# A decoder step on one core: gate pairs in seven block products, with all low parts on VectorE

## The chip, the cores and the metric

The kernel runs on one core of a Trainium2 chip. The metric is the device time of one execution in microseconds, the median of several runs. The engines are TensorE (PE, with its weight load PEld), VectorE (DVE), ScalarE (ACT), GpSimd (POOL) and SyncE (SP), whose queue issues most DMAs.

## The reference

One layer of a hybrid decoder for 576 tokens at once: a prompt of 512 and 8 samples of 8 tokens, with the same weights; D = 1024, D_FF = 2816, float32.

```python
x += 0.5 * gate1 * swiglu(mod(rmsnorm(x)), w_ff1_in, w_ff1_out)      # FF1
x += gate2 * W_out(sum_i sigmoid(gate_i(h)) * proj_i(branch_i(h)))   # mixer: windowed attention, SSD, RG-LRU
x += 0.5 * gate3 * swiglu(mod(rmsnorm(x)), w_ff2_in, w_ff2_out)      # FF2
y = rmsnorm(x)

def swiglu(h, w_in, w_out):
    u, v = jnp.split(h @ w_in, 2, axis=-1)
    return (jax.nn.silu(u) * v) @ w_out
```

`mod` scales and shifts by vectors worked out from the condition c and the 9216 columns of `w_ada`. States and key/value rows are outputs too.

## The kernel before, in words

Activations lie transposed: 128 partitions of D by 576 tokens, in 8 tiles `H` (high part, fp32r) and 8 tiles `L` (low part, value minus H). A float32 product is made of three fp32r ones: `wh*H + wl*H + wh*L`, where `wh` is the weight's cast and `wl` the rest.

The program is one list of `Unit`s, which `run` goes through in order. A Unit is a block of 128 weight columns: up to 8 k tiles x 3 passes x 2 token halves of 288, so 48 matmuls of 128x288 (L342) into a PSUM tile of two banks from the pool `mm` (two such tiles). `run` issues the loads of weights ahead on SP's queue (`load`, L170), `split` casts `wh` on ScalarE (L278) and subtracts `wl` on VectorE, or on POOL for 48 units with `pool=True` (L280); a Unit's result is evicted at the start of the next Unit. Between the k tiles `run` steps lanes: generators of other work, such as `ada` (modulation, 1 MB of `w_ada` and 8 matmuls, L593, a step), `prep` (bias tables), norms, attention and scans. The order of all instructions on each engine is the order in which the program is written.

`ff_units` writes a feed-forward: its 22 blocks of D_FF stand in groups of 8, 8 and 6. For each block there is a u Unit (evicted with silu on ScalarE, L724) and a v Unit (multiplied on VectorE, L732, then `split` into `a` by L180 and L181), then for each group 8 out-projection Units (L707, L712, L713 add to x). The first blocks of FF2 are halved, so that they begin while the norm of the second token half is still running.

## Time and profile before

| | |
|---|---|
| median of 3 runs | 2097.17 us (2095.91 to 2100.96) |
| the profiled execution | 2096.72 us |
| its span, first to last instruction | 2094.9 us |
| mean granted TensorE clock | 0.990 |
| busy: TensorE, VectorE, ScalarE, POOL | 97%, 45%, 40%, 13% |
| the chain that ended last | TensorE 65% of the span, L342 alone 53% |

The chain follows the work back from the last instruction, at each step to what released it. FF1 takes about the first 500 us, the mixer 500 to 1630, FF2 the rest. An operation's time is read from the timeline of its engine; the bracket at the end of such a row is the idle time of the engine before it and what ended it. A clock of 1.00 is 2.4 GHz.

### The profile page before, as it was taken

Reading aid. Unit: us, or ns where it says so; the run is one execution under the profiler, and the core shown is the slowest. Engines: PE = TensorE matmul, PEld = TensorE weight load, DVE = VectorE, ACT = ScalarE, POOL = GpSimd, SP = SyncE. Lnnn points to the kernel's source line nnn. Section 1 sums busy time; section 2 is a strip of 40 time slices with the busy share of each in tenths; the row PEclk is TensorE's granted clock in tenths of the full one; section 3 lists DMA queues with packets and bytes.
Section 4 is the critical chain, followed back from the end, with each engine's and each line's share of the span. In section 5 each row is a group of like instructions: output and inputs, shape, how many; then the busy total and the mean of one; then the engine's idle time right before and its main releaser. Section 6 shows DMA issues by size and latency. Waiting matters only on the chain.

```text
span 2094.9 us, 40560 instructions
## 1 busy us (share of the span) xinstructions
PE 2030.4 (97%) x17104; PEld 1911.1 (91%) x17104; DVE 952.2 (45%) x1759; ACT 832.8 (40%) x1508; POOL 271.6 (13%) x351
## 2 busy tenths in 40 slices
PE   7999999998999999999999989999999999999997
PEld 6888999998998899999999878888989799999997
DVE  4323333337568655225353573434445633333343
ACT  5222222137557446125352646555425522122132
POOL 2000000006003211000003131101136300000002
PEclk8999999999999999999999999999999999999999
DMA  9856322235641485332333185788787422222222
GB/s 276 265 158 209 89 82 81 85 92 152 185 141 54 125 264 174 100 112 60 95 94 99 54 249 183 243 269 284 248 277 229 127 81 81 84 89 81 86 84 68
DMA packets 381088, 304.20 MB, mean 145 GB/s; under 512 B 16176, under 2 KB 329126, under 8 KB 380905
## 3 DMA queue, kind: packets, MB, share of 16 engines
q1 hardware_dynamic: 370888, 271.15, 43.4%
q0 software_dynamic: 10016, 30.44, 4.3%
q8 instruction: 135, 2.21, 0.4%
q14 instruction: 49, 0.39, 0.1%
HBM read 269.88 MB, written 31.66 MB: 144 GB/s over the span
## 4 chain that ended last, share of the span: by engine, by line
PE 65%; DVE 6%; DMA 2%; ACT 2%; issue 1%; SPq 1%; POOL 0%; POOLq 0%; DVEq 0%; ACTq 0%
PE mm L342 53%; PE kt L1735 2%; PE S L1723 1%; PE O L1828 1%; SPq L170 1%; PE px_ld L593 1%; PE px_lru L1889 1%; PE sc L1451 1%; PE po L1507 1%; DVE sq L646 1%; DMA cv<-cache_win_kv 1%; DVE wl L280 1%; DMA ck<-cache_win_kv 1%; PE pt L1490 1%; DVE L L699 0%
## 5 line engine op out<-in xcount | busy, mean ns | idle before, releaser
L342 PE MATMUL mm<-H,wh 128*128 128x288 f32 x4112 | 957.4, 305 | 20.2 <-DVE x L713 9.2
L342 PE MATMUL mm<-L,wh 128*128 128x288 f32 x4112 | 918.7, 296 | 2.6 <-DVE L L181 1.5
L342 PE MATMUL mm<-H,wl 128*128 128x288 f32 x4112 | 917.7, 296 | 0.6 <-POOL wl L280 0.6
L342 PEld LDWEIGHTS mm<-H,wh 128*128 128x128 f32 x4112 | 669.6, 189 | 77.2 <-issue 54.0
L342 PEld LDWEIGHTS mm<-L,wh 128*128 128x128 f32 x4112 | 673.0, 188 | 4.8 <-DVE L L181 2.6
L342 PEld LDWEIGHTS mm<-H,wl 128*128 128x128 f32 x4112 | 673.1, 188 | 1.8 <-POOL wl L280 0.8
L280 DVE TENSOR_TENSOR wl<-raw,wh 128x1024 fp32r<-128x1024 f32 (+1 forms) x241 | 289.9, 1206 | 277.8 <-ACT wh L278 260.1
L278 ACT CAST wh<-raw 128x1024 fp32r<-128x1024 f32 (+2 forms) x289 | 289.7, 1009 | 104.0 <-PE mm L342 94.7
L280 POOL TENSOR_TENSOR wl<-raw,wh 128x1024 fp32r<-128x1024 f32 (+2 forms) x48 | 101.3, 2115 | 722.6 <-ACT wh L278 714.1
L707 DVE SCALAR_TENSOR_TENSOR x<-mm,modT,x 128x288 f32<-128x288 f32 (+1 forms) x112 | 50.9, 480 | 163.3 <-PE mm L342 163.3
L724 ACT ACTIVATE su<-mm 128x576 f32<-128x576 f32 x42 | 27.4, 651 | 238.8 <-PE mm L342 238.8
L180 ACT CAST H<-su 128x576 fp32r<-128x576 f32 x44 | 29.6, 674 | 232.6 <-DVE su L732 226.0
L732 DVE TENSOR_TENSOR su<-su,mm 128x576 f32<-128x576 f32 x42 | 31.7, 754 | 142.4 <-PE mm L342 142.4
L1740 ACT COPY KT<-kt 128x512 f32<-128x512 f32 x78 | 45.5, 587 | 76.5 <-PE kt L1735 65.9
L953 DVE SCALAR_TENSOR_TENSOR acc<-raw,v,acc 128x512 f32<-128x512 f32 x120 | 54.3, 523 | 45.6 <-ACT acc L950 45.4
L1735 PE MATMUL kt<-mats,ck 128*128 128x128 f32 x416 | 64.1, 278 | 9.6 <-DMA ck<-cache_win_kv 7.9
L1735 PEld LDWEIGHTS kt<-mats,ck 128*128 128x128 f32 x416 | 51.3, 143 | 11.9 <-DMA ck<-cache_win_kv 8.2
L1483 ACT ACTIVATE lg<-lg,neg 128x128 f32<-128x128 f32 (+1 forms) x96 | 39.9, 417 | 29.5 <-DVE neg L1474 28.4
L1961 DVE TENSOR_TENSOR sg<-sg,mm 128x576 f32<-128x576 f32 x24 | 18.0, 752 | 68.0 <-PE mm L342 41.7
L181 DVE TENSOR_TENSOR L<-su,H 128x576 fp32r<-128x576 f32 x44 | 33.4, 759 | 32.7 <-ACT H L180 32.7
L641 ACT ACTIVATE sq<-x 128x288 f32<-128x288 f32 x48 | 21.3, 443 | 64.2 <-DVE x L713 32.1
L1738 DVE COPY KT<-kt 128x512 f32<-128x512 f32 x26 | 17.9, 690 | 54.6 <-PE kt L1735 47.2
(388 smaller groups left out, 1720.1 us busy)
## 6 DMA issues: line engine op xcount, KB each, us to landing
raw<-w_in SPq DMA_DIRECT2D x96, 512.0 KB
raw<-w_ff_in SPq DMA_DIRECT2D x88, 512.0 KB
ada<-w_ada SPq DMA_DIRECT2D x72, 512.0 KB
...
```

The costliest lines, as they stand in the source:

```text
L180: self.later(delay[0], lambda: nc.scalar.copy(H, src))
L181: self.later(delay[1], lambda: nc.vector.tensor_tensor(out=L, in0=src, in1=H.bitcast(F32), op=ALU.subtract), L)
L278: nc.scalar.copy(H, r)
L280: self.later(0 if i < 4 else 2, lambda: e.tensor_tensor(out=L, in0=r, in1=H.bitcast(F32), op=ALU.subtract), L)
L342: nc.tensor.matmul(ps[:M, hf, :HALF], wt[:, k, :], x[:, hf * HALF:(hf + 1) * HALF], start=(k == 0 and p == 0), stop=(k == nk - 1 and p == 2))
L707: nc.vector.scalar_tensor_tensor(out=x[:, c0:c0 + n], in0=ps[:, hf, 0:n], scalar=g[:, 0:1], in1=x[:, c0:c0 + n], op0=ALU.mult, op1=ALU.add)
L724: nc.scalar.activation(t.rearrange("p (a b) -> p a b", a=2), ps[:, :, :HALF], AF.Silu)
L732: nc.vector.tensor_tensor(out=tv, in0=tv, in1=ps[:, :, :HALF], op=ALU.mult)
L953: nc.vector.scalar_tensor_tensor(out=o, in0=i, scalar=w[:, k, j:j + 1], in1=o, op0=ALU.mult, op1=ALU.add)
L1483: nc.scalar.activation(e, e, AF.Exp, bias=neg[:, a:a + 1], accum_out=st[:, a, 1, h:h + 1])
L1735: nc.tensor.transpose(ps[:, j * 128:(j + 1) * 128], t[:, q, j * 128:(j + 1) * 128], self.ident)
L1740: nc.scalar.copy(kt, ps)
```

## The change

A new class `Pair` takes the weight blocks b and b+1 of u, or of v, as a 2x2 matrix (the two blocks by the even and the odd k tiles), and the activations as another (even and odd k tiles by the two token halves). Their product is made of seven block products of 4 k tiles x 3 passes = 12 matmuls of 128x288, instead of eight. `operands` makes the seven weight operands: sums of raw blocks (L415), casts on ScalarE (L421) and low parts on VectorE (L415). `products` issues the seven products into four PSUM banks, and VectorE adds across banks (L470). `sums` makes the sums T1, T2 and T3 of the activations with their high and low parts, once in a feed-forward, as a lane (`t0`, `t2`); `overlay` (`o0`, `o2`) then writes T4 over a part of `H` and `L`, before the seventh product of the first Pair.

The groups of a feed-forward are now 4, 6, 6 and 6 blocks. In FF1 two blocks stay plain Units, in FF2 four (two of them halved); the rest are Pairs, 20 in FF1 and 18 in FF2. The pool `mm` has four tiles of one bank, so a Unit's two halves have a bank each, and evictions that took both halves in one operation take two. `pool=` is gone: the 48 low parts that POOL made are VectorE's. A Pair is loaded, cast and subtracted product by product (`prep`, up to five products ahead).

```diff
+class Pair:
+    def __init__(self, wu, wv, xs, evs, lanes=(), drain=()):
+        self.wu, self.wv, self.xs, self.evs, self.lanes, self.drain = wu, wv, xs, evs, lanes, tuple(drain)
+        self.w, self.halves, self.share, self.mate, self.pre = wu, (0, 1), 0, False, None
+        self.key = self.mid = None
+        self.hook = {}
...
-        self.mmp = ctx.enter_context(tc.tile_pool(name="mm", bufs=2, space=PSUM))
+        self.mmp = ctx.enter_context(tc.tile_pool(name="mm", bufs=4, space=PSUM))
...
+            if isinstance(u, Pair):
+                wts[i] = [None] * 7
+                preps.extend((i, n, f) for n, f in enumerate(self.operands(r, wts[i])))
+                return
...
-            e = nc.gpsimd if u.pool else nc.vector
-            self.later(0 if i < 4 else 2, lambda: e.tensor_tensor(out=L, in0=r, in1=H.bitcast(F32), op=ALU.subtract), L)
+            self.later(0 if i < 4 else 2, lambda: nc.vector.tensor_tensor(out=L, in0=r, in1=H.bitcast(F32), op=ALU.subtract), L)
...
+        def prep(i, n, most=7):
+            while n > 6:
+                i, n = i + 1, n - 7
+            while preps and most and preps[0][:2] <= (i, n):
+                preps.pop(0)[2]()
+                most -= 1
...
+                more(16 if isinstance(u, Pair) else 48 if nl == len(units) or isinstance(units[nl], Unit) else 32)
...
+            if isinstance(u, Pair):
+                self.products(u, wts.pop(i), lambda n, most=7: prep(i, n, most), lambda: more(48))
+                continue
...
+    def operands(self, raw, ops):
+        nc = self.nc
+        n = raw[0].shape[1] // 2
+        A11, A12 = raw[0][:, 0::2, :], raw[0][:, 1::2, :]
+        A21, A22 = raw[1][:, 0::2, :], raw[1][:, 1::2, :]
+        src, tmp = {}, {}
+        def tt(o, a, b, op):
+            nc.vector.tensor_tensor(out=o, in0=a, in1=b, op=op)
+        def hi(k, s):
+            t = self.W([2, n, 128], F32R, "op")
+            ops[k] = (t[:, 0], t[:, 1])
+            src[k] = s
+            nc.scalar.copy(ops[k][0], s)
+        def lo(k):
+            tt(ops[k][1], src[k], ops[k][0].bitcast(F32), ALU.subtract)
+        def c0():
+            hi(0, A11)
+            tmp[0] = self.W([n, 128], F32, "s3")
+            tt(tmp[0], A11, A21, ALU.subtract)
+            tt(A21, A21, A22, ALU.add)
+        def c1():
+            lo(0)
+            tt(A11, A21, A11, ALU.subtract)
+            hi(1, A11)
+        def c2():
+            lo(1)
+            hi(2, A21)
+        def c3():
+            lo(2)
+            hi(3, tmp[0])
+        def c4():
+            lo(3)
+            hi(4, A12)
+        def c5():
+            lo(4)
+            tt(A12, A12, A11, ALU.subtract)
+            hi(5, A12)
+        def c6():
+            lo(5)
+            hi(6, A22)
+            self.later(1, lambda: lo(6), ops)
+        return [c0, c1, c2, c3, c4, c5, c6]
+    PRODUCTS = (("B11", 0, True), ("T2", 1, True), ("T1", 3, True), ("T3", 2, True), ("B21", 0, False), ("B22", 3, False), ("T4", 2, False))
+    def products(self, pr, ops, prep, more):
+        nc = self.nc
+        banks = [self.mm(f"mm{n}")[:, :HALF] for n in "bacd"]
+        b, a, c, d = banks
+        u2 = None
+        ev = self.events(pr.lanes)
+        at = 0
+        add = lambda o, x, y: nc.vector.tensor_tensor(out=o, in0=x, in1=y, op=ALU.add)
+        for s, (name, bank, first) in enumerate(self.PRODUCTS):
+            if s:
+                self.flush()
+            prep(min(s + 1, 6))
+            prep(s + 5, 1)
+            if s == 3:
+                more()
+            if s in pr.hook:
+                pr.hook[s]()
+            if s == 6 and any(e[2] == id(ops) for e in self.todo):
+                self.flush(True)
+            xs = pr.xs()
+            WH, WL = ops[s]
+            for q, x in enumerate(xs):
+                xh, xl = x[name]
+                for p, (wt, m) in enumerate(((WH, xh), (WL, xh), (WH, xl))):
+                    nc.tensor.matmul(banks[bank], wt[:, q, :], m, start=first and q == 0 and p == 0,
+                                     stop=q == len(xs) - 1 and p == 2, skip_group_check=True)
+            while at < len(ev) and at * 7 < (s + 1) * len(ev):
+                self.flush()
+                self.step(ev[at], 1)
+                at += 1
+            if s == 0:
+                t = self.B(T, name="u2")
+                u2, p5 = t[:, 0:HALF], t[:, HALF:T]
+                nc.scalar.copy(u2, b)
+            elif s == 1:
+                add(u2, a, u2)
+            elif s == 2:
+                nc.scalar.copy(p5, d)
+                add(d, d, u2)
+            elif s == 3:
+                add(c, c, u2)
+                add(a, c, p5)
+            elif s == 4:
+                pr.evs(0, 0, b)
+                pr.evs(1, 1, a)
+            elif s == 5:
+                pr.evs(0, 1, d)
+            elif s == 6:
+                pr.evs(1, 0, c)
...
+        def ev_uu(b):
+            def f(n, hf, ps):
+                if b + n not in su:
+                    su[b + n] = self.B(name="su")
+                nc.scalar.activation(su[b + n][:, hf * HALF:(hf + 1) * HALF], ps, AF.Silu)
+            return f
+        def ev_vv(b):
+            left = {b: 2, b + 1: 2}
+            def f(n, hf, ps):
+                t = su[b + n][:, hf * HALF:(hf + 1) * HALF]
+                nc.vector.tensor_tensor(out=t, in0=t, in1=ps, op=ALU.mult)
+                left[b + n] -= 1
+                if not left[b + n]:
+                    a[b + n] = self.split(su.pop(b + n), (1, 4 + 2 * n))
+            return f
+        groups = [range(0, 4), range(4, 10), range(10, 16), range(16, 22)]
         units = []
         hk = lambda: self.hh[l]
-        def pair(b, eu=ev_u, ev=ev_v):
+        xs = lambda: self.xs[l]
+        both = tuple((name, 3 if name == "ada" else 2) for name, n in lanes)
+        def pair(b, eu=ev_u, ev=ev_v, lanes=lanes):
             units.append(Unit(self.wview(win, 0, 8, b * 128), hk, eu(b), lanes=lanes))
             units.append(Unit(self.wview(win, 0, 8, 2816 + b * 128), hk, ev(b), lanes=lanes))
-        n = 0
+        def two(b, off, evs):
+            units.append(Pair(self.wview(win, 0, 8, off + b * 128), self.wview(win, 0, 8, off + b * 128 + 128), xs, evs, lanes=both))
         if cover is not None:
             for n in range(2):
-                pair(n, ev_uh, ev_vh)
+                pair(n, ev_uh, ev_vh, lanes=((f"t{l}", 2),))
             units[0].drain = (f"n{l}0",)
             units = self.halved(units, *cover)
-            n = 2
-        for b in groups[0][n:]:
-            pair(b)
+            for n in (2, 3):
+                pair(n, lanes=((f"t{l}", 2),))
+        else:
+            pair(0)
+            pair(1, lanes=lanes[:1] + lanes + ((f"t{l}", 8),))
+        def opening():
+            units[-1].drain = (f"t{l}",)
+            units[-1].lanes += ((f"o{l}", 4),)
+            units[-1].hook[6] = lambda: self.drain(f"o{l}")
+        if cover is None:
+            two(2, 0, ev_uu(2))
+            opening()
+            two(2, 2816, ev_vv(2))
         for n, grp in enumerate(groups):
-            rest = []
-            if n < 2:
-                pair(groups[n + 1][0])
-                rest = groups[n + 1][1:]
-            for halves in (((0, 1),) if n < 2 else ((0,), (1,))):
+            last = n == len(groups) - 1
+            if not last:
+                b0 = groups[n + 1][0]
+                two(b0, 0, ev_uu(b0))
+                if n == 0 and cover is not None:
+                    opening()
+            for halves in (((0,), (1,)) if last else ((0, 1),)):
                 for j in range(8):
                     units.append(Unit(self.wview(wout, grp[0], len(grp), j * 128), (lambda grp=grp: [a[b] for b in grp]),
-                                      ev_o(j, halves, n == 2),
-                                      lanes=lanes if n < 2 else nxt[0] if halves == (0,) else nxt[1] + fill * (j == 2),
-                                      halves=halves, pool=n == 2 and halves == (1,)))
-            for b in rest:
-                pair(b)
+                                      ev_o(j, halves, last),
+                                      lanes=lanes if not last else nxt[0] if halves == (0,) else nxt[1] + fill * (j == 2),
+                                      halves=halves))
+            if not last:
+                two(b0, 2816, ev_vv(b0))
+                for b in range(b0 + 2, groups[n + 1][-1], 2):
+                    two(b, 0, ev_uu(b))
+                    two(b, 2816, ev_vv(b))
         return units
+    def sums(self, l, t):
+        nc = self.nc
+        lo, hi = slice(0, HALF), slice(HALF, T)
+        self.xs[l] = xs = []
+        def sub(o, a, b):
+            nc.vector.tensor_tensor(out=o, in0=a, in1=b, op=ALU.subtract)
+        two = None
+        for q in range(4):
+            e, o = t[2 * q], t[2 * q + 1]
+            (He, Le), (Ho, Lo) = self.hh[l][2 * q], self.hh[l][2 * q + 1]
+            sub(e[:, lo], e[:, hi], e[:, lo])
+            sub(e[:, hi], o[:, hi], e[:, hi])
+            yield
+            sub(o[:, hi], o[:, hi], e[:, lo])
+            H, L = self.B(T, F32R, "H"), self.B(T, F32R, "L")
+            nc.scalar.copy(H, e)
+            if q % 2 == 0:
+                two = (self.B(T, F32R, "H"), self.B(T, F32R, "L"))
+            h = (lo, hi)[q % 2]
+            nc.scalar.copy(two[0][:, h], o[:, hi])
+            yield
+            sub(o[:, lo], o[:, lo], o[:, hi])
+            sub(L, e, H.bitcast(F32))
+            yield
+            sub(two[1][:, h], o[:, hi], two[0][:, h].bitcast(F32))
+            xs.append({"B11": (He[:, lo], Le[:, lo]), "B21": (Ho[:, lo], Lo[:, lo]), "B22": (Ho[:, hi], Lo[:, hi]),
+                       "T1": (H[:, lo], L[:, lo]), "T3": (H[:, hi], L[:, hi]), "T2": (two[0][:, h], two[1][:, h]),
+                       "T4": (He[:, hi], Le[:, hi])})
+            yield
+    def overlay(self, l, t):
+        for q in range(4):
+            H, L = self.xs[l][q]["T4"]
+            self.nc.scalar.copy(H, t[2 * q + 1][:, 0:HALF])
+            yield
+            self.nc.vector.tensor_tensor(out=L, in0=t[2 * q + 1][:, 0:HALF], in1=H.bitcast(F32), op=ALU.subtract)
+        t.clear()
+        yield
...
-        for u in um[:4] + u2[:4]:
-            u.pool = True
```

**VectorE, FF2, between gate blocks.** wl is a Unit's low weights, su the gate product, L the low part of `a`. Before:

```order
L280 TENSOR_TENSOR wl_21231<-raw_21165,wh_21230 128x1024
L732 TENSOR_TENSOR su_21228<-su_21228,mm_21233 128x576
L181 TENSOR_TENSOR L_21287<-su_21228,H_21286 128x576
L280 TENSOR_TENSOR wl_21290<-raw_21225,wh_21289 128x1024
L280 TENSOR_TENSOR wl_21348<-raw_21282,wh_21347 128x1024
```

Of the change, around the border of a v Pair and the u Pair behind it (op is a low part of an operand, raw and s are weight sums, mma to mmd the four banks, u_ the copies u2 and p5):

```order
L941 TENSOR_TENSOR su_22376<-su_22376,mma_22412 128x288
L415 TENSOR_TENSOR op_22492<-raw_22343,op_22492 128x512
L941 TENSOR_TENSOR su_22374<-su_22374,mmd_22414 128x288
L415 TENSOR_TENSOR op_22509<-s_22452,op_22509 128x512
L941 TENSOR_TENSOR su_22376<-su_22376,mmc_22413 128x288
L415 TENSOR_TENSOR op_22528<-raw_22341,op_22528 128x512
L415 TENSOR_TENSOR raw_22341<-raw_22341 128x4x128
L415 TENSOR_TENSOR op_22552<-raw_22341,op_22552 128x512
L470 TENSOR_TENSOR u_22566<-mma_22547,u_22566 128x288
L192 TENSOR_TENSOR L_22525<-su_22374,H_22524 128x576
L415 TENSOR_TENSOR op_22569<-raw_22343,op_22569 128x512
L415 TENSOR_TENSOR s_22588<-raw_22473,raw_22475 128x512
```

Two wl, a product and a low part for two Units became eleven operations of 512, four sums and four products for a v Pair; the low parts of `a` stand among the next Pair's operands.

**TensorE, FF1, from the first product to the second of the first Pair.** Before, such a stretch is one Unit's k tiles:

```order
L342 MATMUL mm_1161<-H_452,wh_1011 128x288 x2
L342 MATMUL mm_1161<-H_452,wl_1012 128x288 x2
L342 MATMUL mm_1161<-L_457,wh_1011 128x288 x2
L342 MATMUL mm_1161<-H_501,wh_1011 128x288 x2
L342 MATMUL mm_1161<-H_501,wl_1012 128x288 x2
L342 MATMUL mm_1161<-L_506,wh_1011 128x288 x2
```

Of the change (mmb and mma are banks, op the weight operands, H_716 and L_717 are T2, px_ld is a step of `ada`):

```order
L487 MATMUL mmb_960<-L_513,op_725 128x288
L487 MATMUL mmb_960<-H_601,op_725 128x288 x2
L487 MATMUL mmb_960<-L_606,op_725 128x288
L750 MATMUL px_ld_757<-ada_867,cT_143 32x512 x2
L750 MATMUL px_ld_757<-ada_871,cT_143 32x512 x2
L487 MATMUL mma_961<-H_716,op_755 128x288 x2
L487 MATMUL mma_961<-L_717,op_755 128x288
```

The second product reads what `sums` made.

**VectorE, start of FF1.** Before, from the first product of a gate block to the second (pmk belongs to `prep`):

```order
L732 TENSOR_TENSOR su_672<-su_672,mm_391 128x576
L181 TENSOR_TENSOR L_690<-su_672,H_689 128x576
L280 TENSOR_TENSOR wl_693<-raw_680,wh_692 128x1024
L280 TENSOR_TENSOR wl_778<-raw_682,wh_777 128x1024
L840 TENSOR_TENSOR pmk_744<-px_prep_822,pmk_744 8x384
L840 TENSOR_TENSOR pmk_748<-px_prep_826,pmk_748 8x384
L840 TENSOR_TENSOR pmk_752<-px_prep_830,pmk_752 8x384
L732 TENSOR_TENSOR su_775<-su_775,mm_780 128x576
L181 TENSOR_TENSOR L_866<-su_775,H_865 128x576
```

Of the change, the first third of what stands between the same two gate products (t are the activations before they are split, and their sums):

```order
L1006 TENSOR_TENSOR t_305<-t_305 128x288
L1006 TENSOR_TENSOR t_305<-t_345,t_305 128x288
L1006 TENSOR_TENSOR t_345<-t_345,t_305 128x288
L415 TENSOR_TENSOR s_727<-raw_688,raw_690 128x512
L415 TENSOR_TENSOR raw_690<-raw_690 128x4x128
L1006 TENSOR_TENSOR t_345<-t_345 128x288
L1006 TENSOR_TENSOR L_714<-t_305,H_713 128x576
L1006 TENSOR_TENSOR L_717<-t_345,H_716 128x288
L415 TENSOR_TENSOR op_725<-raw_688,op_725 128x512
L415 TENSOR_TENSOR raw_688<-raw_690,raw_688 128x4x128
L415 TENSOR_TENSOR op_755<-raw_688,op_755 128x512
L1006 TENSOR_TENSOR t_363<-t_363 128x288
```

The sums of four pairs of k tiles and the first operands now stand between the two blocks' gate products; T2's last low part is 26 rows below the last one shown, ahead of the second gate product.

## Rows read from the trace of the kernel before

**Rows 1.** Busy times on the page: busy us, share of the span, instructions.

```profile
PE 2030.4 (97%) x17104; PEld 1911.1 (91%) x17104; DVE 952.2 (45%) x1759; ACT 832.8 (40%) x1508; POOL 271.6 (13%) x351
```

**Rows 2.** Table by stretches: us, busy us (instructions) by engine, PEclk, DMA share, GB/s.

```profile
88.00:440.00 352.00, 352.00 (x2644) 334.70 (x2637) 114.32 (x180) 84.31 (x105) 4.40 (x8) 1.00 0.41 123
490.00:500.00 10.00, 7.72 (x47) 7.51 (x46) 9.86 (x18) 7.99 (x16) 7.76 (x7) 0.83 0.74 240
500.00:510.00 10.00, 6.92 (x49) 6.37 (x48) 7.26 (x16) 6.21 (x10) 3.93 (x4) 1.00 0.51 149
1550.00:1590.00 40.00, 34.90 (x249) 33.37 (x250) 27.40 (x26) 17.96 (x26) 25.41 (x13) 1.00 0.83 255
1620.00:1640.00 20.00, 15.51 (x103) 13.91 (x103) 19.66 (x35) 14.25 (x26) 11.48 (x5) 0.91 0.57 186
1690.00:2040.00 350.00, 349.33 (x2636) 348.86 (x2635) 121.12 (x167) 83.38 (x104) 2.43 (x2) 1.00 0.29 83
```

**Rows 3.** Timeline of VectorE, FF2's out-projections: start, duration, instruction, idle before.

```profile
1767.72 0.88 DVE L707 SCALAR_TENSOR_TENSOR x<-mm,modT,x 128x288 f32<-128x288 f32 x2 [2.66 <-PE mm L342]
...
1774.06 0.88 DVE L707 SCALAR_TENSOR_TENSOR x<-mm,modT,x 128x288 f32<-128x288 f32 x2 [3.81 <-PE mm L342]
```

**Rows 4.** Timeline of VectorE, FF2's gate units.

```profile
1723.22 0.76 DVE L732 TENSOR_TENSOR su<-su,mm 128x576 f32<-128x576 f32 x1 [3.51 <-PE mm L342]
...
1735.94 0.75 DVE L732 TENSOR_TENSOR su<-su,mm 128x576 f32<-128x576 f32 x1 [3.52 <-PE mm L342]
```

**Rows 5.** VectorE by line and form: count, busy us, mean ns, idle before.

```profile
L280 DVE TENSOR_TENSOR wl<-raw,wh 128x1024 fp32r<-128x1024 f32 x224 | 275.0, 1228 | 263.5 <-ACT wh L278 245.8 <-PE mm L342 4.9 <-DMA ck<-cache_win_kv 3.6
...
L181 DVE TENSOR_TENSOR L<-su,H 128x576 fp32r<-128x576 f32 x44 | 33.4, 759 | 32.7 <-ACT H L180 32.7
```

**Rows 6.** Timeline of VectorE, operations of 512 in a row.

```profile
668.77 0.68 DVE L1129 TENSOR_TENSOR M<-M,cbm 128x512 f32<-128x512 f32 x1
669.37 0.68 DVE L1072 TENSOR_TENSOR xd<-px_xt,bt 128x512 f32<-128x512 f32 x1
```

**Rows 7.** Timeline of VectorE, operations of 288 in a row.

```profile
1628.17 0.45 DVE L694 TENSOR_TENSOR t<-x,rstd 128x288 f32<-128x288 f32 x1
1628.54 0.45 DVE L699 TENSOR_TENSOR L<-t,H 128x288 fp32r<-128x288 f32 x1
```

**Rows 8.** ScalarE by line and form.

```profile
L1740 ACT COPY KT<-kt 128x512 f32<-128x512 f32 x78 | 45.5, 587 | 76.5 <-PE kt L1735 65.9 <-PE S L1723 6.5 <-DVE gc L1928 2.3
```

**Rows 9.** Timeline of VectorE, first products of FF1's gate units.

```profile
56.99 0.75 DVE L732 TENSOR_TENSOR su<-su,mm 128x576 f32<-128x576 f32 x1
...
71.37 0.76 DVE L732 TENSOR_TENSOR su<-su,mm 128x576 f32<-128x576 f32 x1 [2.02 <-PE mm L342]
```

**Rows 10.** Table by stretches, from the one to the other.

```profile
57.00:71.40 14.40, 14.40 (x99) 11.64 (x98) 5.61 (x9) 3.21 (x4) 0.00 (x0) 1.00 0.48 149
```

**Rows 11.** Transfers, 50 to 130 us in 40 slices of 2 us, and their mean.

```profile
GB/s 256 376 401 304 29 80 301 412 49 12 149 193 261 403 347 368 369 343 383 332 392 326 96 258 168 279 313 33 238 153 133 170 185 313 213 151 236 248 207 176
DMA packets 19060, 19.32 MB, mean 241 GB/s; under 512 B 1010, under 2 KB 16534, under 8 KB 19054
```

**Rows 12.** Timeline of VectorE in the a-projection.

```profile
1564.00 0.75 DVE L1961 TENSOR_TENSOR sg<-sg,mm 128x576 f32<-128x576 f32 x1
...
1566.28 2.14 DVE L181 TENSOR_TENSOR L<-sg,H 128x576 fp32r<-128x576 f32 x1 [0.74 <-ACT H L180]
1568.34 0.74 DVE L1961 TENSOR_TENSOR sg<-sg,mm 128x576 f32<-128x576 f32 x1
```

**Rows 13.** Timeline of POOL in the a-projection.

```profile
1564.94 5.71 POOL L280 TENSOR_TENSOR wl<-raw,wh 128x1024 fp32r<-128x1024 f32 x2 [2.98 <-ACT wh L278]
```

**Rows 14.** Timeline of VectorE in the change to FF2.

```profile
1621.08 2.25 DVE L646 TENSOR_TENSOR sq<-sq,sq 128x288 f32<-128x288 f32 x1
...
1623.99 2.64 DVE L694 TENSOR_TENSOR t<-x,rstd 128x288 f32<-128x288 f32 x1
```

More of the change, by code (lines that the diff above doesn't have):

```diff
@@ L308, in run, with more @@
             seen = max(seen, i)
-            end = begin[seen] + u.w.shape[1] * len(u.halves)
+            end = begin[seen] + size(units[seen])
             early = n < len(first) - 2
             tight = any(name in ("sk", "sv") for name, _ in u.lanes) or "sk" in g.drain or n < len(first)
-            while nl < len(units) and (nl <= seen + 2 and not early if tight else begin[nl] < end + 48):
-                load(nl)
-                nl += 1
+            def more(room):
+                nonlocal nl
+                while nl < len(units) and begin[nl] < end + room:
+                    load(nl)
+                    nl += 1
+            if tight:
+                while nl < len(units) and nl <= seen + 2 and not early:
+                    load(nl)
+                    nl += 1
+            else:
+                more(16 if isinstance(u, Pair) else 48 if nl == len(units) or isinstance(units[nl], Unit) else 32)
             while ns <= min(seen + 1, nl - 1) and not early:
@@ L320, in run @@
             for _ in range(0 if tight else 2):
-                if ns < nl and begin[ns] < end + 32:
+                if ns < nl and begin[ns] < end + (32 if isinstance(units[ns], Unit) else 20 if isinstance(u, Unit) else 0):
                     split(ns)
@@ L524, in stage_d @@
             H, L = self.hh[0][j]
[L525 removed]
+            nc.vector.tensor_tensor(out=L, in0=tC[j], in1=H.bitcast(F32), op=ALU.subtract)
+        self.lanes["t0"] = self.sums(0, tC)
+        self.lanes["o0"] = self.overlay(0, tC)
         self.hh[0] = []
@@ L686, in norm_lane @@
         ts = {}
+        if l == 2 and hf == 0:
+            self.t2 = {}
+            self.lanes["t2"] = self.sums(2, self.t2)
+            self.lanes["o2"] = self.overlay(2, self.t2)
         yield
@@ L1287, in f @@
             t = self.B(name="z")
-            self.nc.scalar.copy(t.rearrange("p (a b) -> p a b", a=2), ps[:, :, :HALF])
+            for hf in range(2):
+                self.nc.scalar.copy(t[:, hf * HALF:(hf + 1) * HALF], ps[hf][:, :HALF])
             self.store(self.sgd[:, 24 + j, :], t)
@@ L1860, in f @@
             t = self.B(name="gc")
-            self.nc.scalar.copy(t.rearrange("p (a b) -> p a b", a=2), ps[:, :, :HALF])
+            for hf in range(2):
+                self.nc.scalar.copy(t[:, hf * HALF:(hf + 1) * HALF], ps[hf][:, :HALF])
             self.gc[j] = t
@@ L1942, in f @@
             t = self.B(name="sg")
-            self.nc.scalar.copy(t.rearrange("p (a b) -> p a b", a=2), ps[:, :, :HALF])
+            for hf in range(2):
+                self.nc.scalar.copy(t[:, hf * HALF:(hf + 1) * HALF], ps[hf][:, :HALF])
             self.store(self.sgd[:, n * 8 + j, :], t)
```

95 lines of the change are left out of this document (56 added, 39 removed).

## The prediction

> **What bounds the kernel now.** I read the busy times first: TensorE is busy 2030.4 us, 97% of the span, and no other engine reaches half of it [rows 1]. Then the table by stretches [rows 2]: in 88 to 440 us (most of FF1's gate units and out-projections) TensorE is busy all 352.00 us, in 1690 to 2040 us (FF2) 349.33 of 350, at granted clock 1.00, while VectorE works 114 to 121 us there and ScalarE 83 to 84. So inside the feed-forwards a matmul less is time less, until another engine runs out of room. The same table shows where TensorE is not the bound: the change from FF1 to the mixer (490 to 510 us), the a-projection (1550 to 1590) and the change to FF2 (1620 to 1640).
>
> The price of a matmul: the evictions of two consecutive out-projection units of 48 matmuls start at 1767.72 and 1774.06 us [rows 3], 6.34 us, so **0.1321 us each**. Two gate units lie between the products at 1723.22 and 1735.94 [rows 4]: 12.72 us for 96, 0.1325. A unit border costs nothing as it stands.
>
> **Term 1, products removed.** A `Pair` does two weight blocks in 7 products of 4 k tiles and 3 passes: 84 matmuls instead of 96. FF1 has 20 Pairs (20 of its 22 blocks, u and v), FF2 18; 38 x 12 = 456 matmuls go: 456 x 0.1321 = **-60.2 us**. The out-projections, now in four groups, keep their number of matmuls; the eight updates of x more in each FF lie under TensorE's units as they do now [rows 3].
>
> **Term 2, does the work around a Pair fit under it?** TensorE needs 84 x 0.1321 = 11.1 us for a Pair, 22.2 for a u and a v Pair. On VectorE each Pair has 7 low parts and 4 weight sums of 128x512, and 4 sums of 128x288; a v Pair adds 4 gate products of 128x288 and two low parts of 128x576, which run into the next u Pair. Durations are 0.68, 0.45 and 0.76 us [rows 5 to 7]; operations in a row overlap at their ends, and start 0.60 (512) and 0.37 (288) apart [rows 6, 7]. By starts a u Pair is 11 x 0.60 + 4 x 0.37 = 8.1 us and a v Pair 8.1 + 4 x 0.37 + 2 x 0.76 = 11.1; by durations 9.3 and 12.6. So VectorE goes from about 4 us of 12.7 (two wl, one product, one L [rows 4, 5]) to between 19.2 and 21.9 of 22.2: it fits, narrowly. ScalarE has 7 casts of 512 at 0.59 (by a copy of that size [rows 8]), two copies of 288, and four silus or two casts of 576, some 6 to 7 of 11.1 us: it fits.
>
> What TensorE then waits for: the banks of products 5 to 7 must have been read or summed since their first use. The tightest is product 7, whose bank needs `c+u2` and `a=c+p5`, issued after product 4; it has two products, 3.2 us, for these two (0.9) and for what stands ahead of them in the queue, at most two of 512 (1.4). The operands are made up to five products ahead. Lower bound 0, if each lead holds; upper bound the v Pairs' whole excess by durations, 19 x 1.5 = 28. I take **+3**, near the lower end: u and v together fit by either count, and v's last low parts may run into u.
>
> **Term 3, the start of FF1.** Only four plain units stand ahead of the first Pair, the second of their v units is evicted at 71.37 us [rows 9], and there TensorE would begin the Pair. VectorE's queue from 56.99 on now holds, as the excerpt for this place shows, the work of `sums` (per q five operations of 288 and one of 576, four q: 12.0 us by durations), eleven of 512 for the first operands (7.5), a gate product and its low part (1.7) and the three pmk (1.8): 23.0 us, until 80.0. Between 57 and 71.4 it was busy 5.6 of 14.4 us [rows 10], so the queue doesn't fit ahead of the Pair. TensorE would be through with two products at 71.4 + 3.2 + 0.9 for a step of `ada` (units here take 7.2 us, not 6.34 [rows 3, 9]) = 75.5, and needs T2's last low part for that: 4.5 us late. T4, which `overlay` builds behind this and the drain at product 7 waits for, gives some 2 more. Then the clock: around the waits in 490 to 500 us the granted clock is 0.83 [rows 2], 1.7 us in 10. Bounds 3 (the queue by starts, 20 us) and 16 (twice the count). I take **+8**. In FF2 the sums are spread over four whole blocks' units, over 50 us: nothing.
>
> **Term 4, transfers.** `ada` fetches 1 MB a step, now three steps a Pair. A first Pair thus needs 4 MB in 11.1 us and three steps at 0.9, 13.8 us: 304 GB/s; a plain unit needed 1.5 MB in 7.2, 218. An out-projection unit of 4 k tiles needs 1.25 MB in 4.1 us, 320. The channel gave up to 412 GB/s, and 241 on the mean of 50 to 130 us [rows 11]. Bounds 0 and 8 us (0.5 MB late six times at 412 GB/s); I take **+2**, since weights are asked for a Pair ahead.
>
> **Term 5, low parts from POOL to VectorE.** 48 low parts leave POOL. In 1564 to 1570 us VectorE's L181 takes 2.14 us instead of 0.76 where POOL's low parts run, and the gate products of two units (24 matmuls, 3.17 us) start 4.34 us apart [rows 12, 13]; at 1621 and 1624 two operations of 288 take 2.25 and 2.64 us for 0.45 [rows 7, 14]. The Trainium skill (SBUF — State Buffer, section "SBUF: two separate sides") has a lock on the ports that VectorE and GpSimd share, held for a whole instruction, and a VectorE operation with two inputs in SBUF is blocked by it; these rows agree. Without POOL's low parts the time above 0.76 or 0.45 goes. TensorE's idle is 5.1 us in 1550 to 1590, 4.5 in 1620 to 1640 and 5.4 in 490 to 510 [rows 2]. Against it, each moved low part is up to 1.23 us more on VectorE [rows 5]: in 1620 to 1640 VectorE is already busy 19.65 of 20 us and POOL 11.5 [rows 2], some 4 or 5 low parts, so 5 us come and 1.80 + 2.19 us of holding [rows 14] go. I take -4 in the a-projection and -1 in the two changes: **-5**, bounds -10 and +4.
>
> **Sum.** -60.2 + 3 + 8 + 2 - 5 = -52.2. The profiled execution took 2096.72 us, 0.45 under the median 2097.17: 2096.7 - 52.2 = 2044.5, **2045 us**.
>
> **Rivals.** A: VectorE sets the pace in the v Pairs. For it: 12.6 against 11.1 us by durations; against it: starts 0.60 and 0.37 apart, and the u Pair's free 2 to 3 us. Price 28 instead of 3: 2070.
>
> B: FF1's start and its transfers cost their upper bounds, 24 instead of 10: 2059. For it: stretches near the fullest rate before [rows 11].
>
> C: slower. Each product has a hand-over that TensorE doesn't hide, since its first matmul waits for a bank or operand that another engine has just finished. There are 38 x 7 = 266 products; the 55 us gained without term 2 are gone at 0.21 us each, and at 0.25 the time is 2041.5 + 66.5 = 2108. Against it: a unit border costs nothing [rows 3, 4]; but no border there has banks into which VectorE sums.
>
> D: slower, by the clock. Waits inside the Pairs take it down as in 490 to 500 us: 47 matmuls in 10 us at 0.83, where 88 to 440 us hold 75 per 10 [rows 2], 3.7 us lost. One such stretch a Pair is 38 x 3.7 = 141 us: 2183; from 15 Pairs on it decides. Against it: no such stretch inside the two feed-forwards. The Trainium skill (TensorE: Matmul & The Clock Gate, "A second HAM failure mode: psum-queue depth-cycling") describes short idles between groups of matmuls that cycle through PSUM banks and move the clock down and up again; no row here shows that form, only the drop beside a longer wait.
>
> That the change removes nothing is excluded by the order: 12 matmuls fewer a Pair.
>
> **How the numbers follow.** Forecast (2030 to 2058) 0.62, A 0.14, B 0.14, C 0.06, D 0.02, below 2030 0.02. The range 2030 to 2076 takes in A and B and leaves out C, D and the last. A measurement here tells 0.3%, 6.3 us, from no change. Faster (below 2091): the forecast, A, B and below, less some 0.04 for mixtures in which A grows: 0.88; same 0.05, those mixtures and a mild C; slower 0.07.
>
> **What would show it.** Right: some 456 fewer matmuls of 128x288, TensorE busy over 97% in the gate stretches, a u and a v Pair 22 to 23 us apart with VectorE busy 85 to 95%; a hole of 4 to 8 us at 70 to 90 us; the a-projection's units under 3.6 us apart, without VectorE operations of 2 us. Wrong: waits of TensorE in every Pair that end with VectorE's sums or low parts (A, C), a granted clock below 1.00 inside the feed-forwards (D), weight loads that end last (B).

## The result, and the profile after

The changed kernel takes 2061.37 us (median; 2060.58 to 2063.96, 4 runs) against 2098.57 for the kernel before beside it: ratio 0.982, 95% interval 0.981 to 0.984. It is 37 us faster, 1.8%. The forecast was 2045, 52 us faster, with a range of 2030 to 2076.

The busy times of the kernel after, laid out as in [rows 1]; 456 matmuls are gone, as counted:

```profile
PE 1980.3 (96%) x16648; PEld 1857.4 (90%) x16648; DVE 1242.1 (60%) x2503; ACT 947.9 (46%) x1894; POOL 171.8 (8%) x303
```

The table by stretches, laid out as in [rows 2]:

```profile
280.00:440.00 160.00, 160.00 (x1211) 160.00 (x1210) 128.46 (x238) 68.69 (x135) 0.00 (x0) 1.00 0.33 95
320.00:340.00 20.00, 20.00 (x154) 20.00 (x153) 18.32 (x33) 11.06 (x23) 0.00 (x0) 1.00 0.20 55
480.00:500.00 20.00, 11.00 (x68) 9.77 (x68) 15.85 (x40) 14.78 (x27) 3.06 (x6) 0.81 0.55 170
1540.00:1580.00 40.00, 36.89 (x261) 34.92 (x262) 30.49 (x52) 19.27 (x29) 0.54 (x1) 1.00 0.84 256
1800.00:1980.00 180.00, 180.00 (x1360) 180.00 (x1359) 135.67 (x259) 70.38 (x139) 0.00 (x0) 1.00 0.30 86
```

Where a Pair follows a Pair in a quiet stretch, the change does what was counted. Two gate products at the same place of successive v Pairs (timeline of VectorE, FF2):

```profile
1857.23 0.45 DVE L941 TENSOR_TENSOR su<-su,mmb 128x288 f32<-128x288 f32 x1
...
1879.48 0.45 DVE L941 TENSOR_TENSOR su<-su,mmb 128x288 f32<-128x288 f32 x1
```

They are 22.25 us apart; 168 matmuls at 0.1321 are 22.2. TensorE is without a pause there and in 280 to 440. So what is missing was lost elsewhere. The starts of the updates of x (L707 before, L873 after) and, at the mixer's end, of the last gate product of the a-projection cut the span into stages; each entry is the difference of two such starts in one profile. "Lows on VectorE" and "no Pairs" are experiments below: the kernel before with POOL's 48 low parts moved, and the changed kernel with plain Units for its Pairs.

| stage, us | before | lows on VectorE | no Pairs | after | after, lows on POOL |
|---|---|---|---|---|---|
| start to the first update of FF1's last out-projection | 462.5 | 460.9 | 466.5 | 447.3 | 446.7 |
| FF1's last out-projection | 43.1 | 47.7 | 47.6 | 48.8 | 43.6 |
| mixer to the last gate product of the a-projection | 1075.8 | 1077.3 | 1077.4 | 1076.3 | 1076.9 |
| w_out | 56.5 | 57.9 | 57.3 | 57.3 | 56.4 |
| FF2 to the first update of its last out-projection | 394.4 | 390.8 | 387.4 | 361.9 | 362.6 |
| FF2's last out-projection | 47.6 | 49.3 | 51.9 | 51.3 | 48.8 |
| to the end | 15.0 | 14.8 | 14.8 | 15.9 | 15.2 |

The first stage differs by up to 2 us between profiles for its beginning alone. Read by "no Pairs" against "after", the Pairs gave 25.5 of 28.5 us in FF2 but 19.2 of 31.7 in FF1; and both feed-forwards end later with the low parts on VectorE. What is left of the change beside Pairs and low parts is "no Pairs" against "lows on VectorE": 5.6 us longer in FF1, 3.4 shorter in FF2's first stage, 2.6 longer at FF2's end.

FF1's loss stands in TensorE's timeline of the kernel after (the last row is FF2's); the bracket is the idle time and what ended it:

```profile
77.71 0.53 PE L487 MATMUL mma<-H,op 128*128 128x288 f32 x2 [1.25 <-ACT H L1021]
78.65 0.40 PE L487 MATMUL mma<-L,op 128*128 128x288 f32 x1 [0.41 <-DVE L L1006]
...
190.40 0.53 PE L487 MATMUL mmb<-H,op 128*128 128x288 f32 x2 [1.82 <-ACT su L933]
...
218.67 0.53 PE L487 MATMUL mmb<-H,op 128*128 128x288 f32 x2 [1.82 <-ACT su L933]
...
240.37 0.53 PE L487 MATMUL mmd<-H,op 128*128 128x288 f32 x2 [0.84 <-DVE mmd L470]
...
446.90 0.40 PE L388 MATMUL mm<-L,wh 128*128 128x288 f32 x1 [2.26 <-DVE L L192]
...
1991.31 0.40 PE L388 MATMUL mm<-L,wh 128*128 128x288 f32 x1 [2.28 <-DVE L L192]
```

and the granted clock behind five of these waits (PEclk is the third figure from the end):

```profile
80.00:85.00 5.00, 5.00 (x30) 4.00 (x29) 4.81 (x11) 1.97 (x6) 0.00 (x0) 0.74 1.03 338
...
190.00:195.00 5.00, 4.60 (x24) 4.60 (x25) 2.77 (x4) 3.80 (x10) 0.00 (x0) 0.68 0.00 0
...
220.00:225.00 5.00, 5.00 (x31) 5.00 (x30) 3.47 (x7) 2.61 (x6) 0.00 (x0) 0.74 0.00 0
...
446.90:451.90 5.00, 5.00 (x26) 5.00 (x27) 2.87 (x4) 2.12 (x4) 0.00 (x0) 0.66 0.00 0
...
1990.00:1995.00 5.00, 3.69 (x28) 3.69 (x29) 3.27 (x5) 1.90 (x3) 0.00 (x0) 1.00 0.28 83
1995.00:2000.00 5.00, 5.00 (x40) 5.00 (x39) 3.38 (x6) 2.62 (x5) 0.00 (x0) 1.00 0.29 86
```

At 78 us T2 is late: 1.66 us of waits, and 5 x 0.26 = 1.3 behind them. At 190 and 218 the first product of a v Pair waits for the bank that silu of the u Pair has to read, 3.6 us, and 5 x (0.32 + 0.26) = 2.9 behind them. The first three stretches cut the dips (75 to 80 and 215 to 220 us have 0.92 too, 195 to 200 has 0.97), so each dip is counted 0.1 to 0.4 us low; inside one, in 80 to 82 us, the granted clock is 0.50, the lower level of 1.2 GHz. The out-projection's wait of 2.26 us for the last v Pair's second low part has a dip behind it as well (5 x 0.34 = 1.7); it comes again in FF2 (2.28), and there the clock stays at 1.00. ScalarE's timeline says why silu was late:

```profile
188.01 0.62 ACT L421 CAST op<-raw 128x512 fp32r<-128x512 f32 x1 [4.63 <-DVE raw L415]
188.65 1.28 ACT L933 ACT_TABLE_LOAD   x1
189.94 0.41 ACT L933 ACTIVATE su<-mmb 128x288 f32<-128x288 f32 x1
```

ScalarE stood for 4.63 us at a cast that waited for a weight sum on VectorE, with the silus behind it, and then loaded silu's table, since `prep` had used another function between.

### The profile page after: what moved, and what is told of

It reads as the page before. It is cut to its first block, busy times and chain, and to the rows that moved or that the text cites. A ratio compares the mean times of both kernels' runs of the same rounds, so it can differ in the third digit from the quotient of the medians.

```text
span 2058.9 us, 40902 instructions
## 1 busy us (share of the span) xinstructions
PE 1980.3 (96%) x16648; PEld 1857.4 (90%) x16648; DVE 1242.1 (60%) x2503; ACT 947.9 (46%) x1894; POOL 171.8 (8%) x303
## 5 line engine op out<-in xcount | busy, mean ns | idle before, releaser
L388 PE MATMUL mm<-H,wh 128*128 128x288 f32 x2896 | 695.5, 309 | 5.3 <-ACT H L675 2.3
L388 PE MATMUL mm<-L,wh 128*128 128x288 f32 x2896 | 659.6, 296 | 10.5 <-DVE L L192 6.0
L388 PE MATMUL mm<-H,wl 128*128 128x288 f32 x2896 | 658.0, 296 | 0.9 <-DVE wl L301 0.9
L388 PEld LDWEIGHTS mm<-H,wh 128*128 128x128 f32 x2896 | 475.7, 189 | 55.6 <-issue 41.5
L388 PEld LDWEIGHTS mm<-L,wh 128*128 128x128 f32 x2896 | 478.1, 188 | 13.1 <-DVE L L192 6.9
L388 PEld LDWEIGHTS mm<-H,wl 128*128 128x128 f32 x2896 | 478.5, 189 | 2.1 <-DVE wl L301 1.2
L301 DVE TENSOR_TENSOR wl<-raw,wh 128x1024 fp32r<-128x1024 f32 (+2 forms) x229 | 248.4, 1092 | 160.0 <-ACT wh L300 128.7
L421 ACT CAST op<-raw 128x512 fp32r<-128x512 f32 x228 | 135.5, 620 | 271.8 <-DVE raw L415 222.3
L415 DVE TENSOR_TENSOR op<-raw,op 128x512 fp32r<-128x512 f32 x228 | 155.5, 686 | 30.2 <-ACT op L421 28.0
L487 PE MATMUL mmd<-H,op 128*128 128x288 f32 x608 | 125.8, 299 | 1.7 <-DVE mmd L470 1.6
L873 DVE SCALAR_TENSOR_TENSOR x<-mm,modT,x 128x288 f32<-128x288 f32 (+1 forms) x144 | 65.0, 480 | 101.7 <-PE mm L388 101.7
```

The costliest lines, as they stand in the source:

```text
L301: self.later(0 if i < 4 else 2, lambda: nc.vector.tensor_tensor(out=L, in0=r, in1=H.bitcast(F32), op=ALU.subtract), L)
L388: nc.tensor.matmul(ps[hf][:M, :HALF], wt[:, k, :], x[:, hf * HALF:(hf + 1) * HALF], start=(k == 0 and p == 0), stop=(k == nk - 1 and p == 2))
L415: nc.vector.tensor_tensor(out=o, in0=a, in1=b, op=op)
L421: nc.scalar.copy(ops[k][0], s)
L487: nc.tensor.matmul(banks[bank], wt[:, q, :], m, start=first and q == 0 and p == 0, stop=q == len(xs) - 1 and p == 2, skip_group_check=True)
L873: nc.vector.scalar_tensor_tensor(out=x[:, c0:c0 + n], in0=ps[hf][:, 0:n], scalar=g[:, 0:1], in1=x[:, c0:c0 + n], op0=ALU.mult, op1=ALU.add)
```

## The experiments

**1. The low parts alone, in the kernel before.**

```diff
-            e = nc.gpsimd if u.pool else nc.vector
+            e = nc.vector
```

Expected: 

> The kernel before, with nothing changed but the engine of POOL's 48 low parts: all on VectorE, no Pair. The prediction's term 5 says 5 us faster than before (about 2093). The theory after the result, that low parts on VectorE close a loop at the end of each feed-forward (x's update, its square on ScalarE, the next weight's cast there, its low part on VectorE, the next update: 2.62 us a half unit in the trace after, where 18 matmuls take 2.38), says: FF1's end and FF2's end 3 us longer each, the a-projection 1 and FF2's start 4 us shorter: between 2 us slower and 2 us faster than before, 2097 to 2101.

Measured: 2103.06 us against 2097.32, ratio 1.003 (1.0015 to 1.0044): slower, by 6 us, where the term was -5. The theory's 2097 to 2101 missed as well, on the other side. VectorE was indeed held no longer. The squares' sum (line L646), before and in this run:

```profile
L646 DVE TENSOR_TENSOR sq<-sq,sq 128x288 f32<-128x288 f32 x40 | 38.0, 951 | 0.6
...
L646 DVE TENSOR_TENSOR sq<-sq,sq 128x288 f32<-128x288 f32 x40 | 18.0, 450 | 0.6
```

That is 20 us less in this line alone, against 24 x 1.226 + 16 x 0.956 + 8 x 0.685 = 50 us of new low parts. The busy times of this run show the whole:

```profile
PE 2031.1 (97%) x17104; PEld 1908.6 (91%) x17104; DVE 958.5 (46%) x1807; ACT 833.0 (40%) x1508; POOL 170.1 (8%) x303
```

VectorE's time rose only from 952.2 [rows 1] to 958.5 us, so some 44 us of holding ended, nearly what the new operations take. VectorE is idle for more than half of the span, so its sum says little; experiment 3 looks at where the operations stand in its queue. FF1's end grew by 4.6 us, FF2's end by 1.7; FF2's first stage fell by 3.6 and the a-projection's eight units from 28.2 to 26.4.

**2. The low parts back on POOL, in the changed kernel.** `pool=` as in the kernel before, for the same 48 weights.

Expected: 

> The changed kernel with the same 48 low parts back on POOL (the Pairs and all else kept). The loop theory says: both ends 3 us shorter, FF2's start 4 and the a-projection 1 us longer: 2059 to 2063, about no change. The prediction's term 5 says 5 us slower, 2066.

Measured: 2052.55 us, ratio to before 0.979 (0.978 to 0.980) where the changed kernel has 0.982: 9 us faster than the changed kernel (7.6 if each is compared with the kernel before that was measured beside it); both numbers missed. FF1's end is 5.2 us shorter and FF2's 2.5, as the loop has it, but FF2's first stage is only 0.7 longer, not 4: without Pairs something else of the change, perhaps the one-bank tiles, had already shortened it (390.8 to 387.4, experiment 8). No run has the tiles alone.

**3. Only those of the two ends.**

```diff
+                                      halves=halves, pool=last and halves == (1,)))
```

Expected: 

> The changed kernel with only the 16 low parts of the last eight half units' weights in FF1 and in FF2 back on POOL, the other 32 on VectorE. The loop theory says 6 to 8 us faster, 2053 to 2055, with TensorE's wait for the last square at FF2's end (3.4 us) and at FF1's end (5.7) mostly gone. If the ends are long only because the last v Pair's second low part is late: no change, 2061.

Measured: 2056.09 us, 5.3 faster than the changed kernel (4.0 by the kernel before beside each), less than expected; FF1's end 45.0 us, FF2's 49.0. The loop can be read near FF2's end in the timelines of VectorE and, in two rows, of ScalarE. After:

```profile
2001.36 0.51 DVE L873 SCALAR_TENSOR_TENSOR x<-mm,modT,x 128x288 f32<-128x288 f32 x1
2001.79 0.45 DVE L803 TENSOR_TENSOR sq<-sq,sq 128x288 f32<-128x288 f32 x1
2001.90 0.44 ACT L798 ACTIVATE sq<-x 128x288 f32<-128x288 f32 x1 [1.46 <-DVE x L873]
2002.25 0.82 ACT L300 CAST wh<-raw 128x768 fp32r<-128x768 f32 x1
2003.11 0.96 DVE L301 TENSOR_TENSOR wl<-raw,wh 128x768 fp32r<-128x768 f32 x1 [0.87 <-ACT wh L300]
2003.98 0.51 DVE L873 SCALAR_TENSOR_TENSOR x<-mm,modT,x 128x288 f32<-128x288 f32 x1
```

and with these low parts on POOL:

```profile
1996.46 0.51 DVE L875 SCALAR_TENSOR_TENSOR x<-mm,modT,x 128x288 f32<-128x288 f32 x1
1996.89 1.68 DVE L805 TENSOR_TENSOR sq<-sq,sq 128x288 f32<-128x288 f32 x1
1998.49 0.50 DVE L875 SCALAR_TENSOR_TENSOR x<-mm,modT,x 128x288 f32<-128x288 f32 x1
```

With wl on VectorE an update waits for wl, wl for its cast on ScalarE, the cast for a square there, the square for the update before: 2.62 us a round, with no engine full, where TensorE needs 18 x 0.1321 = 2.38. Without wl in the round the updates come 2.03 us apart, though VectorE's square sum is held to 1.68 by POOL. TensorE itself doesn't wait during these rounds; it pays behind them, in its wait for the square at the end of the row (TensorE, after and in this run):

```profile
2013.38 1.18 PE L2381 MATMUL px_ss<-ones,sq 128*96 128x1 f32 x12 [3.42 <-DVE sq L803]
...
2009.70 0.67 PE L2383 MATMUL px_ss<-ones,sq 128*96 128x1 f32 x6 [0.82 <-DVE sq L805]
```

The expectation's other half missed: FF1's wait for the last square stayed (5.7 and 5.8 us), and so did a second one of 1.4 us in FF2. Why is not shown: the second halves' updates come 4.3 us apart in FF1 in both kernels, but experiment 2, where they come 2.7 and 6.2 apart, has the wait too (6.3).

**4. The last low part first.**

```diff
-                    a[b + n] = self.split(su.pop(b + n), (1, 4 + 2 * n))
+                    a[b + n] = self.split(su.pop(b + n), (0, 1) if b == 20 and n else (1, 4 + 2 * n))
```

Expected: 

> The changed kernel with one order changed: the second low part of the last v Pair of each feed-forward is issued at once behind its product, ahead of the out-projection's first low weights, instead of behind two of them. The late-low theory says the two waits of 2.3 us in front of the last out-projections go, and the clock's dip behind them: 4.6 to 8 us faster, 2053 to 2057. The loop theory says that the ends are set by the loop of ScalarE and VectorE, which starts with the first update: 2 to 5 us faster, since the first update comes 2.3 us sooner each time, and the waits for the last squares stay or grow.

Measured: 2060.1 us, 1.3 less than the changed kernel; the ratio to before is 0.982 for both, so no gain can be told. The wait in front of FF1's last out-projection is now

```profile
PE mm L388 <- DVE L L192: 0.9, 1, 0.9
```

instead of 2.26 (FF2's alike), but the two ends still last 48.5 and 51.3 us. The loop decides there, as that theory said, and the wait of 3.42 us at FF2's end grew to 4.14; the 2 to 5 us that it expected did not come.

**5. Silu's table early.** In `products`, at product 4:

```diff
+                    nc.scalar.activation(tab, self.eps, AF.Silu)
```

Expected: 

> The changed kernel with one silu of 128x1 more on ScalarE at product 4 of those u Pairs that carry lanes (FF1's, and FF2's first), ahead of the operand's cast, so that ScalarE loads silu's table there and not in front of the first eviction. In the trace after, TensorE waits 1.82 us twice in FF1 for the bank that silu frees (190 and 218 us), and the granted clock is 0.68 and 0.74 in the 5 us behind them. If the table's load of 1.28 us is the cause: both waits under 0.6 us, no dip, 2 x 1.28 + 2.9 = 5 us faster, 2056. If the cast that waits for VectorE ahead of the silus in ScalarE's queue is the cause: the waits stay and the time is 2060 to 2062.

Measured: 2059.62 us (2055.6 to 2061.7), 1.8 less; the interval overlaps that of the changed kernel. The waits did what the table's theory said; here they are in TensorE's timeline, with a new one:

```profile
192.04 0.53 PE L490 MATMUL mmb<-H,op 128*128 128x288 f32 x2 [0.40 <-ACT su L936]
206.15 0.51 PE L490 MATMUL mmb<-H,op 128*128 128x288 f32 x2 [1.51 <-DVE su L944]
...
218.89 0.53 PE L490 MATMUL mmb<-H,op 128*128 128x288 f32 x2 [0.41 <-ACT su L936]
```

The clock is 1.00 in all of 180 to 230 us. So the table load was the cause of 1.4 us of each of these two waits. The dips are less certain: in experiment 2 the first wait is as long, and the clock behind it stays at 1.00, with the late gate product of VectorE behind that:

```profile
189.77 0.54 PE L489 MATMUL mmb<-H,op 128*128 128x288 f32 x2 [1.82 <-ACT su L935]
203.88 0.51 PE L489 MATMUL mmb<-H,op 128*128 128x288 f32 x2 [1.50 <-DVE su L943]
...
190.00:195.00 5.00, 5.00 (x39) 5.00 (x39) 3.83 (x6) 3.80 (x9) 0.00 (x0) 1.00 0.00 0
```

Experiments 3 and 4 show the same. The wait of 1.5 us is thus not the silu's doing: it stands wherever the dip at 190 us doesn't, and the changed kernel, with the dip, has only 0.2 us of it. And `prep`'s transfers ended waits of 2.6 us at 126 to 156 us where they had ended 1.5. Part of the gain was given back to them, and part to VectorE's queue, which was as late and had been hidden by the dip.

**6. Four plain blocks ahead in FF1.** `pair(n)` for blocks 2 and 3 too, with the sums' 16 steps over six Units; 18 Pairs.

Expected: 

> The changed kernel with four plain blocks instead of two ahead of FF1's Pairs: 18 Pairs instead of 20, 24 matmuls more (3.2 us), and the activations' sums spread over six Units. If the sums cost what the trace after shows at 78 us (1.66 us of waits and 5 us at clock 0.74, 3.0 us together): 2061, no change. If they cost the 8 us of the prediction's term 3: 2056. The waits at 75 to 80 us must be gone in both cases.

Measured: 2060.35 us: no change. TensorE doesn't wait at all in 60 to 100 us, at clock 1.00:

```profile
60.00:80.00 20.00, 20.00 (x138) 14.23 (x137) 11.14 (x21) 5.00 (x9) 0.00 (x0) 1.00 0.76 253
80.00:100.00 20.00, 20.00 (x149) 16.91 (x148) 10.76 (x23) 6.42 (x13) 0.00 (x0) 1.00 0.75 246
```

So the sums' place cost about the 3.2 us of the 24 matmuls that were added, not 8. (`prep`'s transfers, 1.5 us in the changed kernel, end no wait in this one either, so these two together cost about that.)

**7. More on VectorE in each Pair.** Two times `add(t, t, t)` of 128x576, at products 5 and 6.

Expected: 

> The changed kernel with two more operations of 128x576 on VectorE in each Pair (at products 5 and 6, on a tile that nothing reads any more; 0.67 us each by starts, 51 us in all). VectorE is busy 18.0 to 18.3 of 20 us in 280 to 340 us after the change, 20.2 for a u and a v Pair of 22.2 us. If VectorE has that room and only its sum counts: 20.2 + 2.7 = 22.9, 0.7 us too much 19 times: 13 us slower, 2075. If it is already the pace-setter (rival A), or each hand-over is on the path (rival C): all of it, 2100 to 2112. If the queue has more room than its busy time shows: 2061 to 2064.

Measured: 2089.8 us, 28 more than the changed kernel, of 51 us put on VectorE: 0.75 us a Pair, between the expectations. (By stages the feed-forwards up to their last out-projections are 13.8 and 12.0 us longer, 0.68 a Pair; the mixer, which has no Pair, was 4.9 longer in this profile.) TensorE now waits inside the Pairs (by stretch, then the waits of TensorE in 1740 to 2000 us by line):

```profile
320.00:340.00 20.00, 18.36 (x137) 17.93 (x136) 18.52 (x33) 10.09 (x22) 0.00 (x0) 1.00 0.32 93
```

```profile
PE mmd L487 <- DVE mmd L470: 4.6, 5, 1.9
PE mmc L487 <- DVE mma L470: 2.9, 5, 0.8
```

VectorE is at 18.52 of 20 us, hardly more than before the addition (18.3). Rival A was not the case, but its border is less than 1.3 us a Pair away.

**8. No Pairs.** Each Pair as two plain Units, without `sums`; all else as changed.

Expected: 

> The changed kernel with each Pair written as two plain Units of the same blocks, and without the sums of the activations; groups, banks of one, evictions by halves and VectorE's low parts as changed. It tells the Pairs' worth from that of all the rest. If the rest beside the low parts is worth nothing, it takes what the kernel before with its low parts on VectorE took, 2103, and the Pairs are worth 42 of the 60.2 us counted. If the one-bank tiles help the half units at FF2's start (361.9 us after, 390.8 there, of which the Pairs explain 28.5), it is 2100; if four groups and two evictions a Unit cost, 2106 to 2112.

Measured: 2104.4 us (ratio 1.003, 1.002 to 1.005). The Pairs are worth 2104.4 - 2061.4 = 43 us of 60.2. The rest of the change is the 6 us of experiment 1, and some 1 us that can't be told from nothing, though by stages it is a loss in FF1 and a gain in FF2.

**9 and 10. The repairs together.** The second with all 48 low parts on POOL, the first with the a-projection's 8 on VectorE, and both with experiments 4 and 5.

Expected: 

> The changed kernel with three repairs together: 40 of the 48 low parts back on POOL (all but the a-projection's 8, whose units were 1.5 us shorter in all with VectorE), the last v Pair's second low part issued at once, silu's table loaded early. Taken one by one they gave 8.8 (with the a-projection on POOL), 1.3 and 1.8 us; the loop at the feed-forward's end is open with POOL's low parts, so the 2.3 us wait ahead of it should count in full now. Sum: 2052.5 - 1.5 - 1.3 to 4.6 - 1.8 to 5: 2042 to 2048. If the repairs overlap in the same idle time: 2050 to 2053.

Expected: 

> As the run beside it, but with all 48 low parts on POOL, the a-projection's too. By the stage times it is 1.5 us slower than the run beside it, since the a-projection's gate products wait again for VectorE operations that POOL's low parts hold: 2044 to 2050. If the 8 low parts on VectorE only move the wait elsewhere: the same time.

Measured: 2052.82 us (ratio 0.978, 0.976 to 0.981) and 2050.14 us (0.977, 0.975 to 0.980). The sum of 2042 to 2048 missed; 2050 to 2053, for repairs that overlap, held. The second is the best version found, 11 us under the changed kernel and 49 under the one before beside it. The order of the two is against the stage times. Of the 4.1 us between the two profiles, 3.1 lie in FF1, where the two programs are the same: 444.8 and 441.7 us to the first update of the last out-projection, with waits of 1.85 and 1.56 us for `prep`'s transfers and a dip at 80 us in the first alone. The mixer takes 1078.2 and 1078.0, so whether the a-projection's low parts belong on POOL stays open. Over experiment 2 the two order repairs give 2.4 us by the times and 4.6 by the kernel before beside each, and the intervals overlap. FF1's last wait is as long as ever in it:

```profile
488.50 1.32 PE L820 MATMUL px_rstd<-sq,ones 128*128 128x288 f32 x2 [6.33 <-DVE sq L808]
```

## Why the prediction was right, and where it was off

The direction and the range held, for the reason given: TensorE was the bound, its matmuls went, and VectorE's queue in a Pair just fits. But 2061 lies above the forecast's own band (2030 to 2058), in the part of the range that rivals A and B had brought in, and neither of them happened: experiment 7 shows room left in VectorE's queue, and FF1's start and transfers cost about 3.0 + 1.5 us, not B's 24. That the time is close to B's 2059 is chance. The change gave 37.2 us where 52.2 were forecast (the kernel before took 1.4 us more in these runs than in those that the forecast started from). So the centre was too low, and the step that failed is **term 5**.

**Term 1** (-60.2): right. A u and a v Pair take 22.25 us, and no stretch shows another price of a matmul.

**Term 2** (+3): VectorE's share was read rightly (18.3 of 20 us in 320 to 340, 92%), but the term is too small, and its check of ScalarE was wrong in kind. "some 6 to 7 of 11.1 us: it fits" adds up durations; the order in the queue decided. In FF1 a table load of 1.28 us behind a cast that waited for VectorE stood in front of 3.6 us of waits and, in this trace, 2.9 of clock (experiment 5 takes each wait from 1.82 to 0.4). The hand-overs that I had looked at, the sums in front of products 6 and 7, cost 0.84 and twice 0.44 in FF1 and 0.73 in FF2. The low part of the last v Pair, 2.3 us in each feed-forward, I had allowed to "run into u"; but behind the last v Pair comes no u Pair.

**Term 3** (+8): the hole is at the place forecast, and 3.0 us long. TensorE waited 1.25 us for T2's cast and 0.41 for its low part, not 4.5: it came at 76.5 us, not 75.5, and the low part was done at 78.6, not 80.0. `overlay` cost no wait. By durations I had counted the queue as if every operation stood alone; the bound by starts was nearer.

**Term 4** (+2): weights ended no wait of TensorE in FF1 from 60 us on. `prep`'s own transfers ended three at 130 to 152 us, 1.5 us together; before the change there was none.

**Term 5** (-5): measured +5.7 alone (experiment 1) and +8.8 in the changed kernel (experiment 2; 7.6 by the kernel before beside each). I had counted the time in which POOL's low parts held VectorE as what would come back, and the new operations only in 1620 to 1640 us (where VectorE's 19.65 us should read 19.66). In the a-projection the holds went, but the units' products, which were to come under 3.6 us apart, are still 4.16 apart (timeline of VectorE, after):

```profile
1560.04 0.81 DVE L2214 TENSOR_TENSOR sg<-sg,mm 128x288 f32<-128x288 f32 x2
1560.89 0.76 DVE L2216 TENSOR_TENSOR sg<-m,sg 128x576 f32<-128x576 f32 x1
1562.39 0.76 DVE L192 TENSOR_TENSOR L<-sg,H 128x576 fp32r<-128x576 f32 x1 [0.74 <-ACT H L191]
1563.06 1.22 DVE L301 TENSOR_TENSOR wl<-raw,wh 128x1024 fp32r<-128x1024 f32 x1
1564.20 0.81 DVE L2214 TENSOR_TENSOR sg<-sg,mm 128x288 f32<-128x288 f32 x2
```

wl's 1.14 us stands where the hold of 1.4 us stood [rows 12]. The Trainium skill (SBUF — State Buffer, section "SBUF: two separate sides") has a GpSimd instruction hold the shared ports against a VectorE operation with two inputs in SBUF, and the trace agrees: 951 ns beside POOL's low parts, 450 without. But the new operations stand in the queue that was held. At the ends of the feed-forwards they closed the loop of experiment 3, which the text did not look for; opening it there gave 5.3 of the 8.8 us. Where the rest lies is not shown.

Together: the Pairs removed 60 us and lost 17 of them (experiment 8), where terms 2 to 4 had 13; the low parts cost 6 (experiment 1), where term 5 had -5. That is 4 and 11 of the 15 us that the forecast missed. The sum of -60, 17 and 6 meets the measured -37 by construction, since the three come from differences between the same kernels; by experiment 2 the low parts' share is larger and the Pairs' smaller. Of the 17, the waits and dips named above are 3.0 + 6.5 + 2.5 + 4.6 us. That they nearly add up is in part luck: the last of these is partly covered by the loop, as experiment 4 shows, the dip behind 446.9 us and `prep`'s 1.5 us are not among them, and the kernel without Pairs has waits of its own (2.67 us at 487 us, 3.74 at 2057). Rivals C and D did not come: two Pairs of 38 had a dip in the clock behind them, beside the first. The dips followed waits of 1.66, 1.82 and 2.26 us; behind waits of 0.84 (240 us) and 1.51 (experiment 5) the clock stayed at 1.00, but so it did behind the 2.28 us in FF2 and behind one of the two waits of 1.82 in experiment 2. What decides is not shown. The Trainium skill (TensorE: Matmul & The Clock Gate, "A second HAM failure mode: psum-queue depth-cycling") describes short idles between groups that make the clock swing between its two levels; here most borders between products had no idle, and the trace doesn't show that form.
